# Attention's softmax sums: from a broadcast by matmul to a broadcast read back from DRAM

## The chip, the cores and the metric

The kernel runs on one core of a Trainium2 chip. A core has a matmul engine (TensorE, PE in the profile), three elementwise engines (VectorE is DVE, ScalarE is ACT, GpSimd is POOL) and a sync engine (SP) that here only issues DMA transfers. Each engine runs its own list of instructions in the order that was fixed when the program was built, and waits for the others through semaphores. The time is device microseconds (us) of one execution.

## The reference

Two layers over 1024 tokens of width 1024. Layer 0 mixes tokens with grouped-query attention (16 heads of 64, 4 key/value heads), layer 1 with a gated MLP over chunks; each is followed by a squared-ReLU MLP. The change lies in the end of the attention:

```python
s = jnp.einsum('bqkgd,bskd->bkgqs', q_blk, k).astype(jnp.float32) * scale
p = jax.nn.softmax(s, axis=-1).astype(v.dtype)
return jnp.einsum('bkgqs,bskd->bqkgd', p, v)
...
return o @ w_o
...
x = x + g1[:, None, :] * y
```

## The kernel before, in words

Activations are held transposed: width on the 128 partitions, in eight tiles `dt` (or `m`, `k`) of 128, and tokens along the free axis, in two halves `hf` of 512. Every large product is three matmuls: an operand is split into a high part (a cast to a shorter float, on ACT) and a low part (the rest, a subtraction on DVE or POOL), and high·high, high·low and low·high are added up in PSUM.

**Attention** runs as 64 units, one for each head and each 256 queries, in a software pipeline: at step `i` PE makes the scores of unit `i` (L948), transposes the exponentials of unit `i-1` (L965) and multiplies those of unit `i-1` and `i-2` with the values (L984). DVE takes the row maximum (L951) and the low parts (L974), ACT the exponentials (L957, which add up the row sums in `rowsum`) and the high parts (L968), POOL adds the two parts of a unit's output (L1001). These instructions are kept in program order by `pin`. The others, such as most of what is named below, are placed by the scheduler of the language, which moves an instruction among its neighbours as its readiness and the buffers allow. The exponentials are not divided by their sum at once. The unnormalized output of a head pair and half, `ot[(dt, hf)]` (128 x 512), is multiplied by the reciprocal sums later, in `wo_prep`. In between, at the `m` place of a unit, side work runs: the slabs (L184 to L200: weights loaded by SP, multiplied and summed on POOL) and `mod_ahead` (a weight column loaded on SP, L221, multiplied with the condition and summed on DVE one to two units later, L225).

**The reciprocal sums** in the kernel before: `wo_sums(hf)` takes the reciprocal of the 128 x 64 sums (L880), splits it in high and low (L882, L883), transposes it four times on PE into a 32 x 512 tile (L886), and ACT copies that out of PSUM (L888). `wo_prep(hf, dt)` then multiplies a 0/1 matrix `sel` with it on PE (L892), which puts each head's row on its 64 partitions in PSUM; DVE multiplies the attention output with that (L894), ACT takes the high part (L896) and POOL (first half) or DVE (second half) the low part (L897). `sel` is loaded (L869) and cast on ACT (L875) before. For the first half all this is spread over the units 53 to 62, one `dt` in each unit from 55 on; for the second half it stands between the output products.

**The output projection**, `wo_mm(m, halves, bank)`, has 24 matmuls for a half (L906 to L908), then DVE adds the gated result to `x` (L910), ACT squares it (L260) and DVE sums the squares (L264). Its weights come through `issue_w`: SP loads a tile of 128 x 1024 (L113), ACT casts the high part (L116), POOL subtracts for the low part (L117). `AHEAD = 1`, so `wo_mm(m)` issues the weights of `m + 1`: those that `wo_mm(3)` needs are asked for in `wo_mm(2)`. `WA = 6`: after the attention come `wo_mm(1)` to `wo_mm(5)` for the first half, `wo_mm(6)` and `(7)` for both, then `wo_mm(0)` to `(5)` for the second. `mods(n)` adds column loads with a multiplication on DVE (L145, L153) between them.

## Time and profile before

| | |
|---|---|
| time, median of 3 runs | 2628.07 us (2626.15 to 2628.24) |
| span of the profiled execution | 2625.8 us |
| PE busy | 2601.6 us, 99% of the span |
| DVE, ACT, POOL busy | 83%, 55%, 28% |
| granted TensorE clock, mean | 0.999 |
| units 53 to 63 and the end of attention | from about 470 to 555 us |
| output projection around the change | from about 548 to 582 us |

The profile is of one execution. Its span runs from the first to the last instruction; the median of the runs lies 2.3 us above it. Rows of the timeline begin with the start in us and the length in us, then engine, line, operation, output <- inputs, the number of instructions, and in brackets how long the engine had been idle before, and for what. Rows of the grouped views say busy us, mean ns of one, and idle time before.

### The profile page before, as it was taken

How to read it: one execution, taken by the hardware profiler on the slowest of the kernel's cores; microseconds unless marked ns; L12 is line 12 of the kernel's file. 1: busy time of each engine (PE TensorE's matmuls, PEld its weight loads, DVE VectorE, ACT ScalarE, POOL GpSimd, SP SyncE). 2: the span in 40 equal slices, each digit the busy share in tenths (PEclk: the TensorE clock that was granted, in tenths of full speed). 3: DMA queues.
4: the chain of work that ended last, by engine and by line, in shares of the span. 5: the costliest groups of instructions: out<-in, count | busy, mean ns of one | idle time of the engine just before them, and what ended most of it. 6: DMA issues, size and time to landing. Idle time of an engine off the chain costs nothing. (4 is left out here: it accounts for less than half of the span.)

```text
span 2625.8 us, 37307 instructions
## 1 busy us (share of the span) xinstructions
PE 2601.6 (99%) x12860; PEld 2172.2 (83%) x12860; DVE 2183.1 (83%) x3276; ACT 1451.1 (55%) x2612; POOL 723.2 (28%) x531
## 2 busy tenths in 40 slices
PE   9999999999999999999999999999999999999999
PEld 7789999888788888888888888888888788888887
DVE  7868999887989989877897687788979977789974
ACT  4569999854654455446543354445456645465442
POOL 0238776533000004430122054451520000005400
PEclk9999999999999999999999999999999999999999
DMA  8010222234486788545243355568641554487461
GB/s 306 27 33 9 74 88 75 97 112 145 168 288 245 270 310 306 192 133 172 82 136 121 120 174 175 178 204 305 237 141 50 177 179 156 153 310 268 149 211 58
DMA packets 208752, 435.39 MB, mean 166 GB/s; under 512 B 23025, under 2 KB 35441, under 8 KB 208562
## 3 DMA queue, kind: packets, MB, share of 16 engines
q1 hardware_dynamic: 181682, 395.24, 44.7%
q10 hardware_dynamic: 26880, 37.76, 4.0%
q8 instruction: 102, 1.67, 0.3%
q14 instruction: 88, 0.72, 0.1%
HBM read 310.23 MB, written 122.68 MB: 165 GB/s over the span
## 5 line engine op out<-in xcount | busy, mean ns | idle before, releaser
L1212 PE MATMUL out<-t,s 128*128 128x512 f32 x1232 | 479.9, 390 | 0.9 <-ACT t L328 0.8
L1213 PE MATMUL out<-t,s 128*128 128x512 f32 x1232 | 479.3, 389 | 0.7 <-DVE t L329 0.7
L1214 PE MATMUL out<-t,s 128*128 128x512 f32 x1232 | 478.9, 389 | 0.0
L469 PE MATMUL w<-t,s 128*128 128x512 f32 x1168 | 459.8, 395 | 0.9 <-ACT t L328 0.5
L470 PE MATMUL w<-t,s 128*128 128x512 f32 x1168 | 455.2, 390 | 1.8 <-DVE t L329 1.8
L471 PE MATMUL w<-t,s 128*128 128x512 f32 x1168 | 454.7, 389 | 0.0
L329 DVE TENSOR_TENSOR t<-t,t 128x512 fp32r<-128x512 f32 x408 | 324.7, 806 | 36.2 <-ACT t L328 29.0
L328 ACT CAST t<-t 128x512 fp32r<-128x512 f32 x408 | 245.3, 617 | 122.2 <-DMA t<-hf 71.7
L1213 PEld LDWEIGHTS out<-t,s 128*128 128x128 f32 x1232 | 231.2, 188 | 50.2 <-DVE t L329 1.8
L1212 PEld LDWEIGHTS out<-t,s 128*128 128x128 f32 x1232 | 231.2, 188 | 50.2 <-ACT t L328 1.7
L1214 PEld LDWEIGHTS out<-t,s 128*128 128x128 f32 x1232 | 231.2, 188 | 48.1
L454 ACT CAST s<-w 128x512 fp32r<-128x512 f32 x292 | 173.4, 616 | 161.4 <-PE w L471 104.3
L470 PEld LDWEIGHTS w<-t,s 128*128 128x128 f32 x1168 | 219.3, 188 | 49.7 <-DVE t L329 5.2
L469 PEld LDWEIGHTS w<-t,s 128*128 128x128 f32 x1168 | 219.3, 188 | 49.4 <-issue 2.9
L471 PEld LDWEIGHTS w<-t,s 128*128 128x128 f32 x1168 | 219.2, 188 | 45.6
L455 DVE TENSOR_TENSOR s<-w,s 128x512 fp32r<-128x512 f32 x292 | 221.8, 766 | 41.1 <-ACT s L454 40.6
L1194 ACT CAST s<-t 128x512 fp32r<-128x512 f32 x240 | 148.2, 620 | 187.0 <-PE out L1214 136.3
L1180 POOL TENSOR_TENSOR w<-w,t 128x512 f32<-128x512 f32 x20 | 34.2, 1721 | 767.7 <-DMA t<-hf 691.5
L1195 DVE TENSOR_TENSOR s<-t,s 128x512 fp32r<-128x512 f32 x240 | 195.1, 814 | 56.1 <-ACT s L1194 55.4
L951 DVE TENSOR_REDUCE mx<-s 128x1 f32<-128x1024 f32 x128 | 156.2, 1220 | 30.5 <-PE s L948 29.2
L974 DVE TENSOR_TENSOR t<-t,t 128x512 fp32r<-128x512 f32 x256 | 164.1, 681 | 17.1 <-ACT t L968 16.4
L984 PE MATMUL o<-t,t 128*128 128x256 f32 x1024 | 162.6, 291 | 0.0
(251 smaller groups left out, 5089.1 us busy)
## 6 DMA issues: line engine op xcount, KB each, us to landing
t<-hf SPq DMA_DIRECT2D x320, 256.0 KB, 4.0
hf<-c SPq DMA_DIRECT2D x156, 256.0 KB, 3.4
w<-in_wi_dram SPq DMA_DIRECT2D x64, 512.0 KB, 4.5
hf<-c ACTq DMA_DIRECT2D x96, 256.0 KB, 2.7
w<-in_ada_dram SPq DMA_DIRECT2D x36, 512.0 KB, 3.9
x<-in_ada_dram SPq DMA_DIRECT2D x64, 256.0 KB, 5.4
t<-in_wm_dram SPq DMA_DIRECT2D x64, 256.0 KB, 4.7
wf<-w SPq DMA_DIRECT2D x64, 256.0 KB, 3.0
```

Source lines behind the costliest of these rows:

```text
L328: S.copy(hi, src)
L329: (eng or V).tensor_tensor(lo, src, f32(hi), ALU.subtract)
L454: S.copy(hi, src)
L455: V.tensor_tensor(lo, src, f32(hi), ALU.subtract)
L469: T.matmul(ps, hi[:, a], th, start=kt == 0, stop=False)
L470: T.matmul(ps, hi[:, a], tl, start=False, stop=False)
L471: T.matmul(ps, lo[:, a], th, start=False, stop=kt == 3)
L974: pin(V.tensor_tensor(lo, pt, f32(hi), ALU.subtract))
L1195: V.tensor_tensor(lo, src, f32(hi), ALU.subtract)
L1212: T.matmul(ps, hi[:, a], th, start=begin and kt == 0, stop=False, **g)
L1213: T.matmul(ps, hi[:, a], tl, start=False, stop=False, **g)
L1214: T.matmul(ps, lo[:, a], th, start=False, stop=end and kt == 3, **g)
```

## The change

The broadcast by matmul goes. `wo_sums` keeps the reciprocal in one float32 piece, transposes it four times into a 16 x 512 tile, copies it on ACT and stores it from ACT's queue to a DRAM tile `rd`. A new function `wo_load(hf, dt)` issues two loads on SP's queue, each of which reads one row of `rd` for 64 partitions. `wo_prep` multiplies with that tile, which lies in SBUF and not in PSUM. `sel`, its load and its casts are gone. In the first half `wo_sums` moves from unit 54 to unit 49, the loads stand in units 51 to 58, and the products stay in units 55 to 62. In the second half the loads of a group of `dt` stand behind `wo_mm(m)`, and the products ahead of `wo_mm(m + 1)` and no longer of `wo_mm(m)`.

```diff
     def wo_sums(hf):
         ri = small.tile([P, 4, NH], F32, tag="ri", name=nm("ri"), bufs=1)
         V.reciprocal(ri, rowsum[:, 4 * hf : 4 * hf + 4])
-        rs = small.tile([P, 4, 2, NH], F32R, tag="rs", name=nm("rs"), bufs=1)
-        V.tensor_copy(rs[:, :, 0], ri)
-        V.tensor_tensor(rs[:, :, 1], ri, f32(rs[:, :, 0]), ALU.subtract)
-        pt = bank_x("rt", (32, 512), F32R)
+        pt = bank_x("rt", (NH, 512))
         for j in range(4):
-            T.transpose(pt[:, j * P : (j + 1) * P], rs[:, j].rearrange("p s h -> p (s h)"), identr)
-        rT[hf] = slot(F32R, (32, 512))
-        S.copy(rT[hf], f32(pt))
+            T.transpose(pt[:, j * P : (j + 1) * P], ri[:, j], ident)
+        rT = slot(F32, (NH, 512))
+        S.copy(rT, pt)
+        rd[hf] = dram.tile([NH, 512], F32, name=nm("rd"))
+        nc.scalar.dma_start(rd[hf], rT)
+
+    def wo_load(hf, dt):
+        rb_[(dt, hf)] = slot()
+        for i in range(2):
+            nc.sync.dma_start(rb_[(dt, hf)][64 * i : 64 * i + 64],
+                              rd[hf][2 * dt + i : 2 * dt + i + 1].broadcast_to([64, 512]))
 
     def wo_prep(hf, dt):
-        pb = bank_x("bc")
-        T.matmul(pb, sel[dt // 4][:, (dt % 4) * P : (dt % 4 + 1) * P], rT[hf], start=True, stop=True)
         o_ = ot.pop((dt, hf))
-        V.tensor_tensor(o_, o_, pb, ALU.mult)
+        V.tensor_tensor(o_, o_, rb_.pop((dt, hf)), ALU.mult)
...
                     if i in deferred:
                         deferred.pop(i)()
-                    elif i == WO_AT - 6:
-                        load_sel()
-                    elif WO_AT <= i < WO_AT + 10:
-                        if i == WO_AT:
-                            copy_sel()
-                        elif i == WO_AT + 1:
-                            wo_sums(0)
-                        else:
+                    elif i == WO_AT - 4:
+                        wo_sums(0)
+                    elif WO_AT - 2 <= i < WO_AT + 10:
+                        if i < WO_AT + 6:
+                            wo_load(0, i - WO_AT + 2)
+                        if i > WO_AT + 1:
                             wo_prep(0, i - WO_AT - 2)
...
     for m in range(1, WA):
         if m == 1:
             x[1] = [load_x(1, k) for k in range(KT)]
-        for dt in PREP[m - 1] if m < 4 else ():
+        for dt in PREP[m - 2] if 1 < m < 5 else ():
             wo_prep(1, dt)
         wo_mm(m, (0,), bank_y)
+        for dt in PREP[m - 1] if m < 4 else ():
+            wo_load(1, dt)
         mods(WOM[m])
```

Most line numbers move by it: L880 becomes L868, L886 L871, L888 L873, L894 to L897 become L885 to L888, L906 to L910 L897 to L901, L116 and L117 L117 and L118, L225 L226, L260 and L264 L261 and L265, L951 L942, L974 L965. New are the store L875 and the loads L880.

The scheduler places what is not pinned anew, so two places that the diff doesn't name change their order.

The first is DVE's list in attention, in unit 47. In the kernel before, this stands there at a row maximum of that unit (`mx_5500`), with the multiplication of the column that `mod_ahead` loads into `w_5581` two units behind it:

```order
L974 TENSOR_TENSOR t_5476<-t_5467,t_5472 128x512
L951 TENSOR_REDUCE mx_5500<-s_5495 128x1
L974 TENSOR_TENSOR t_5521<-t_5507,t_5512 128x512
L951 TENSOR_REDUCE mx_5537<-s_5532 128x1
L974 TENSOR_TENSOR t_5539<-t_5523,t_5528 128x512
L974 TENSOR_TENSOR t_5548<-t_5541,t_5546 128x512
```

```order
L974 TENSOR_TENSOR t_5702<-t_5686,t_5691 128x512
L974 TENSOR_TENSOR t_5711<-t_5704,t_5709 128x512
L974 TENSOR_TENSOR t_5726<-t_5717,t_5722 128x512
L225 SCALAR_TENSOR_TENSOR w_5581,mod<-w_5581,s_110 128x1024
L226 TENSOR_TENSOR mod<-mod,cols 128x1
L166 SCALAR_TENSOR_TENSOR amod<-mod,cols 128x1
```

Now the same place reads so (the column is named `w_5579` here):

```order
L965 TENSOR_TENSOR t_5478<-t_5469,t_5474 128x512
L942 TENSOR_REDUCE mx_5502<-s_5497 128x1
L226 SCALAR_TENSOR_TENSOR w_5579,mod<-w_5579,s_112 128x1024
L965 TENSOR_TENSOR t_5523<-t_5509,t_5514 128x512
L942 TENSOR_REDUCE mx_5539<-s_5534 128x1
L965 TENSOR_TENSOR t_5541<-t_5525,t_5530 128x512
```

The column's multiplication (L225, now L226) has moved up, from behind the three low parts of a later unit to right behind the row maximum `mx_5502`, ahead of a low part that attention waits for.

The second place is the output projection, on ACT. `wo_mm(2)` adds to `x_6947` (now `x_6948`), and `wo_mm(3)` uses the weights `s_7226` (now `s_7206`), `wo_mm(4)` `s_7280` (now `s_7270`), `wo_mm(5)` `s_7320` (now `s_7326`). Before:

```order
L896 CAST t_7140<-t_4466 128x512
L896 CAST t_7147<-t_4634 128x512
L896 CAST t_7154<-t_4804 128x512
L116 CAST s_7226<-w_7224 128x1024
L260 ACTIVATE t_7190<-x_6945 128x512
L896 CAST t_7206<-t_4968 128x512
L896 CAST t_7213<-t_5148 128x512
L116 CAST s_7280<-w_7278 128x1024
L896 CAST t_7220<-t_5316 128x512
L260 ACTIVATE t_7256<-x_6947 128x512
L896 CAST t_7267<-t_5486 128x512
L116 CAST s_7320<-w_7318 128x1024
```

Now:

```order
L261 ACTIVATE t_7167<-x_6946 128x512
L887 CAST t_7190<-t_4468 128x512
L887 CAST t_7195<-t_4636 128x512
L887 CAST t_7200<-t_4806 128x512
L261 ACTIVATE t_7236<-x_6948 128x512
L117 CAST s_7206<-w_7204 128x1024
L887 CAST t_7254<-t_4970 128x512
L887 CAST t_7259<-t_5150 128x512
L887 CAST t_7264<-t_5318 128x512
L117 CAST s_7270<-w_7268 128x1024
L261 ACTIVATE t_7300<-x_6950 128x512
L887 CAST t_7315<-t_5488 128x512
```

The cast of the weights for `wo_mm(3)` stood ahead of the square of `x_6945`, the result of `wo_mm(1)`. Now it stands behind the square of `x_6948`, the result of `wo_mm(2)`. In the rows behind these the cast for `wo_mm(5)` likewise stands behind the square of `wo_mm(4)`'s result.

The third is DVE's list at the same place. Before:

```order
L894 TENSOR_TENSOR t_4466<-t_4466,bc_7137 128x512
L894 TENSOR_TENSOR t_4634<-t_4634,bc_7144 128x512
L894 TENSOR_TENSOR t_4804<-t_4804,bc_7151 128x512
L897 TENSOR_TENSOR t_7141<-t_4466,t_7140 128x512
L897 TENSOR_TENSOR t_7148<-t_4634,t_7147 128x512
L897 TENSOR_TENSOR t_7155<-t_4804,t_7154 128x512
L910 SCALAR_TENSOR_TENSOR x_6945<-wo_7164,mod,x_6945 128x512
```

Now:

```order
L901 SCALAR_TENSOR_TENSOR x_6946<-wo_7141,mod,x_6946 128x512
L265 TENSOR_TENSOR t_7060<-t_7060,t_7167 128x512
L885 TENSOR_TENSOR t_4468<-t_4468,t_7170 128x512
L901 SCALAR_TENSOR_TENSOR x_6948<-wo_7210,mod,x_6948 128x512
L888 TENSOR_TENSOR t_7191<-t_4468,t_7190 128x512
L885 TENSOR_TENSOR t_4636<-t_4636,t_7173 128x512
L885 TENSOR_TENSOR t_4806<-t_4806,t_7176 128x512
L888 TENSOR_TENSOR t_7196<-t_4636,t_7195 128x512
L888 TENSOR_TENSOR t_7201<-t_4806,t_7200 128x512
```

The products of the first three tiles stood ahead of the addition of `wo_mm(1)`'s result (L910, `x_6945`); now two of the three stand behind that of `wo_mm(2)` (L901, `x_6948`).

## The prediction

> **What bounds the kernel now.** I read the page first, then the waits of PE over the whole span, then the timeline around the change.

> ```profile
> span 2625.8 us, 37307 instructions
> PE 2601.6 (99%) x12860; PEld 2172.2 (83%) x12860; DVE 2183.1 (83%) x3276; ACT 1451.1 (55%) x2612; POOL 723.2 (28%) x531
> ```

> PE is busy 99% of the span. What leaves PE's list is a gain where PE has enough to eat, and whatever makes PE wait is a loss in full, since nothing behind it has slack. The waits of PE (us in total, times, longest) are small:

> ```profile
> PE t L965 <- ACT c L957: 2.4, 3, 1.9
> PE qkv L575 <- DVE t L635: 2.1, 1, 2.1
> PE wo L908 <- POOL s L117: 0.2, 1, 0.2
> ```

> In the output projection PE waited 0.2 us for weights once. So the question is what PE loses in matmuls, and what it gains in waits.

> **What the change removes.** The first term is the eight broadcasts of the first half. PE's timeline has a unit without one (from 470.09 to 475.60) and a unit with one (from 513.15 to 519.58), which also has a transpose of queries:

> ```profile
> 470.09 1.09 PE L948 MATMUL s<-x,t 128*128 128x512 f32 x4
> 475.60 1.09 PE L948 MATMUL s<-x,t 128*128 128x512 f32 x4
> ...
> 513.15 1.20 PE L948 MATMUL s<-x,t 128*128 128x512 f32 x4
> 515.00 0.53 PE L934 MATMUL qt<-identr,t 128*128 128x128 f32 x4
> 515.38 0.62 PE L965 MATMUL t<-ident,c 128*128 128x128 f32 x4
> 519.15 0.49 PE L892 MATMUL bc<-t,t 32*128 32x512 f32 x1
> 519.58 1.20 PE L948 MATMUL s<-x,t 128*128 128x512 f32 x4
> ```

> 6.43 - 5.51 - 0.38 for the query transposes is 0.54 us a broadcast, 4.3 us for eight. But ACT is nearly full in these units. The stretch 508 to 527 (the columns are stretch, length, and busy us of PE, weight loads, DVE, ACT and POOL, then granted clock and DMA) holds 2.95 such units:

> ```profile
> 508.00:527.00 19.00, 19.00 (x134) 16.68 (x133) 16.62 (x22) 17.90 (x36) 6.01 (x6) 1.00 0.26 84
> ```

> ACT idles 1.10 us there, 0.37 a unit; when PE gives back more, ACT sets the pace. So 8 x 0.37 = 3.0 us, with 2.4 (0.3 a unit, not all idle time being usable) and 4.3 as bounds. **-3.0.**

> The two casts of `sel` go from ACT. They stood ahead of a copy of the query transposes for which PE idled 0.33 us: **-0.3.**

> ```profile
> 477.33 1.14 ACT L875 CAST t<-t 32x512 fp32r<-32x512 f32 x2
> ```

> ```profile
> 479.62 0.66 PE L965 MATMUL t<-ident,c 128*128 128x128 f32 x4 [0.33 <-ACT t L937]
> ```

> Unit 57 has the longest wait of attention: ACT stood 2.27 us before the first weight cast, whose load had not landed, and PE ran out of exponentials. Behind it the clock was halved.

> ```profile
> 497.85 1.05 ACT L116 CAST s<-w 128x1024 fp32r<-128x1024 f32 x1 [2.27 <-DMA w<-in_wo_dram]
> ```

> ```profile
> 500.55 1.59 PE L965 MATMUL t<-ident,c 128*128 128x128 f32 x7 [1.89 <-ACT c L957]
> ```

> ```profile
> 115.06:118.47 3.41, 3.41 (x10) 2.64 (x9) 3.41 (x5) 0.08 (x1) 3.25 (x4) 0.50 0.00 0
> 500.77:504.18 3.41, 3.41 (x14) 2.92 (x13) 1.40 (x3) 3.40 (x7) 3.41 (x7) 0.50 0.46 119
> ```

> The two longest waits of PE, 2.1 and 1.89 us, were both followed by 3.41 us at half clock, worth up to 1.7 us each. In the new order both casts stand a few instructions later, so part of this goes: all of it is 1.89 + 1.7 = 3.6, nothing is the other bound. I take **-1.5**.

> In the second half the matmuls stand in three groups (3, 3 and 2) between the output products, with nothing to hide behind. The middle one:

> ```profile
> 562.11 0.39 PE L908 MATMUL wo<-t,s 128*128 128x512 f32 x1
> 562.43 0.96 PE L892 MATMUL bc<-t,t 32*128 32x512 f32 x3
> 563.32 0.51 PE L906 MATMUL wo<-t,s 128*128 128x512 f32 x1
> 563.67 0.40 PE L907 MATMUL wo<-t,s 128*128 128x512 f32 x1
> 563.90 0.40 PE L908 MATMUL wo<-t,s 128*128 128x512 f32 x1
> ```

> From 562.11 to 563.67 two steps took 1.56 us instead of 2 x 0.23: 1.10 us. Three groups: **-3.3**. The transposes of the sums are four before and after. Removed in all: 8.1 us, between 6.0 and 11.5.

> **What it moves.** Two new orders cost PE time. The first is the column's multiplication in attention, which now follows the row maximum directly.

> ```profile
> 438.06 0.35 SPq L221 DMA_DIRECT2D w<-in_ada_dram  x1
> ```

> ```profile
> w<-in_ada_dram SPq DMA_DIRECT2D x1, 512.0 KB, 4.2
> ```

> ```profile
> 438.50 0.69 DVE L974 TENSOR_TENSOR t<-t,t 128x512 fp32r<-128x512 f32 x1
> 453.51 1.22 DVE L225 SCALAR_TENSOR_TENSOR w<-w,s 128x1024 f32<-128x1024 f32 x1
> ```

> ```profile
> 440.28 0.60 PE L965 MATMUL t<-ident,c 128*128 128x128 f32 x4
> ```

> Its column is issued at 438.06 and lands 4.2 us later, at 442.3; before, it was used at 453.5. DVE would stand until then, multiply until 443.5, and finish the low part of 438.50 at 444.2 and not 439.2. PE's transposes at 440.28 to 440.6 need the PSUM bank which that low part reads, so PE waits 3.5 us or so: between 2.7, with a landing 0.8 us sooner, and 5.5, if a POOL addition holds DVE off as below. After a wait of this length the clock fell both times: 1.5 more. **+5.0**, from 2.7 to 7.2.

> The second, and the largest term, is the weights of the output projection. What the parts take there, from the groups by line between 543 and 600 us:

> ```profile
> L117 POOL TENSOR_TENSOR s<-w,s 128x1024 fp32r<-128x1024 f32 x6 | 16.1, 2676 | 30.4 <-ACT s L116 25.5 <-PE bc L892 4.8
> L116 ACT CAST s<-w 128x1024 fp32r<-128x1024 f32 x6 | 6.3, 1051 | 14.8 <-DMA w<-in_wo_dram 8.5 <-PE wo L907 6.3
> L910 DVE SCALAR_TENSOR_TENSOR x<-wo,mod,x 128x512 f32<-128x512 f32 x8 | 6.0, 744 | 3.9 <-PE wo L908 3.9
> L897 DVE TENSOR_TENSOR t<-t,t 128x512 fp32r<-128x512 f32 x8 | 5.3, 683 | 0.0
> L896 ACT CAST t<-t 128x512 fp32r<-128x512 f32 x8 | 4.9, 621 | 6.4 <-DVE t L894 6.4
> L260 ACT ACTIVATE t<-x 128x512 f32<-128x512 f32 x7 | 4.4, 634 | 9.4 <-DVE x L910 9.2
> ```

> Count from the end of `wo_mm(2)`. DVE adds its result (0.74), takes a low part and multiplies two tiles (three at about 0.63 when they follow each other); ACT casts the last tile (0.62), squares (0.63), and only then casts the weights of `wo_mm(3)` (1.05): 4.9 us, in which PE has nothing, because `wo_mm(3)` is next in its list. Then POOL makes the low part (2.4 in the row at 563.49 below) while PE has two matmuls of 0.23: 1.95 more. 6.9 us. For `wo_mm(4)` the cast stands behind three more casts of products that DVE reaches late; by the same rows its high part comes as `wo_mm(3)` ends, and the low part 1.95 later: 2.0. For `wo_mm(5)` it stands behind the square of `wo_mm(4)`: 0.74 + 0.63 + 1.05 = 2.4, and 1.95: 4.4. **+13.3.** The lower bound is 11: neighbours overlap by 0.1 each, and the wait of `wo_mm(4)` halves. The upper is 16: POOL takes the mean of 2.68 each time, and the high part for `wo_mm(4)` comes 2 us late.

> These waits are as long as those after which the clock fell. A half-clock stretch is partly spent in the next wait, so I count 2.0 for three of them, from 0 to 5. **+2.0.** [...]

> The product now reads two SBUF tiles. DVE instructions of that kind stretch where POOL subtracts:

> ```profile
> 564.40 2.05 DVE L264 TENSOR_TENSOR t<-t,t 128x512 f32<-128x512 f32 x1
> ```

> ```profile
> 563.49 2.42 POOL L117 TENSOR_TENSOR s<-w,s 128x1024 fp32r<-128x1024 f32 x1 [4.83 <-PE bc L892]
> ```

> An instruction of this size takes 0.68 otherwise (L897 above); this one lasted until POOL's ended, to within 0.6 us. The products stand in just that chain. [...] One such meeting on the chain costs up to 1.4, and not every one lies on it: **+0.8**, from 0 to 2.7.

> The store and the 32 new loads cost nothing by themselves. In the first half they are issued two units and more ahead of their product. In the second the reciprocals leave ACT where L888 stood; with 2.7 us for a store from ACT's queue and under 4 for a load of SP's, all three tiles land before `wo_mm(2)` ends. What that cover is worth is a rival below.

> ```profile
> hf<-c ACTq DMA_DIRECT2D x96, 256.0 KB, 2.7
> t<-hf SPq DMA_DIRECT2D x320, 256.0 KB, 4.0
> ```

> **The sum.** -8.1 + 5.0 + 13.3 + 2.0 + 0.8 = +13.0 us. On the span of 2625.8 that is 2638.8; the median of the runs lies 2.3 above the span, so 2641.

> **The rivals.** First, the waits are shorter and the clock stays: -8.1 + 2.7 + 12 = +6.6, 2635. For it speaks that a half-clock stretch has been seen only twice; against it, that both times the wait was shorter than these.

> Second, the broadcasts through DRAM come late. A product whose tile has not landed holds DVE, behind it the low parts, and then PE. SP issues in order, and in the second half its loads of broadcasts and of weights stand in one queue; a landing 2 us later in each of the three groups gives +6 more, 2647. Against it: the margin of about 3 us in the second half and of two units in the first.

> Third, the other side: the work taken from PE decides. If the weights' casts were still ready when `wo_mm(3)` to `(5)` begin, only -8.1 would be left, 2620, or 2625 with the wait in attention. The point from which it decides is 8.1 us: the new waits together must stay under that. For it speaks that PE is the bound; against it, that the cast waits in ACT's list for a result which PE itself gives just ahead of needing it. No timing can hide that.

> **Chances.** Forecast 0.62, first rival 0.16, second 0.12, third 0.10. A change within 0.2% (5.3 us) is about what a measurement here can't tell from none: the third rival falls on both sides of it, and the low end of the first reaches into it. Faster 0.07, same 0.09, slower 0.84. The terms' bounds, not all at one end at once, give 2633 to 2650; taking in part of the rivals, the range is 2629 to 2651.

> **What would show it.** In the changed profile: PE waiting on the cast of the weights (L117) some 5 us once and 2 to 3 us once, and on POOL's low part (L118) about 2 us three times; PE waiting near 440 us for a low part (L965), with DVE idle before L226 for its DMA; half clock behind these; units 55 to 62 shorter by 0.3 to 0.4 us with ACT full. It is wrong if PE's waits in the projection add up to less than 8 us, or if DVE waits for the broadcast loads.

## The result, and the profile after

| | before | changed |
|---|---|---|
| median | 2627.11 us (2623.98 to 2628.24, 4 runs) | 2650.55 us (2647.84 to 2652.16, 4 runs) |
| ratio to before, 95% interval | | 1.0089 (1.0078 to 1.0101) |
| span of the profiled execution | 2625.8 us | 2646.1 us |

The change makes the kernel 0.9% slower, 23.4 us by the medians. The forecast was 2641 us. The profiled execution of the changed kernel is its shortest (2647.84 us), 20.3 us of span above that of before; the accounts below are made between these two. One execution of e4 below took 3232.91 us at a mean granted clock of 0.752, and its median leaves it out.

The page's first part and the waits of PE over the span, of the changed kernel:

```profile
span 2646.1 us, 37342 instructions
PE 2601.1 (98%) x12844; PEld 2173.4 (82%) x12844; DVE 2193.1 (83%) x3272; ACT 1449.3 (55%) x2610; POOL 724.7 (27%) x531
```

```profile
PE t L956 <- DVE t L965: 13.1, 8, 5.2
PE wo L897 <- ACT s L117: 9.4, 2, 7.0
PE wo L899 <- POOL s L118: 3.3, 3, 1.7
```

PE has 16 matmuls fewer and is busy as long as before, since its busy time is also longer where the clock is halved (a matmul of the output projection shows 0.63 us there and 0.39 otherwise). The wait for the weights' casts is new. That for POOL's low parts was 0.2 us before, and that for low parts in attention, now 13.1, was this:

```profile
PE t L965 <- DVE t L974: 2.9, 4, 1.1
```

Between 430 and 610 us there was none of it before; 10.2 of the 13.1 lie there now, in four waits. The columns of the next rows are stretch, length, busy us of PE, weight loads, DVE, ACT and POOL, then granted clock and DMA:

```profile
441.40:448.20 6.80, 3.54 (x15) 3.35 (x16) 5.72 (x7) 2.36 (x5) 1.50 (x1) 0.50 0.21 77
564.95:577.52 12.57, 5.60 (x25) 4.32 (x24) 8.78 (x15) 4.05 (x6) 0.00 (x0) 0.88 0.90 271
577.52:587.32 9.80, 8.53 (x25) 6.36 (x25) 8.87 (x13) 2.78 (x4) 4.59 (x2) 0.63 0.70 227
587.32:595.98 8.66, 5.92 (x26) 4.25 (x24) 6.69 (x11) 3.44 (x5) 0.86 (x1) 1.00 0.32 114
595.98:605.10 9.12, 7.42 (x25) 5.70 (x25) 7.66 (x10) 1.04 (x1) 4.84 (x2) 0.81 0.61 184
```

The last four are `wo_mm(2)` to `wo_mm(5)`, from first matmul to first matmul of the next. They take 40.15 us; before, with the broadcasts between them, these four took 22.77. The clock was halved for 6.8 us near 441, for 10.2 from 574.5 and for 3.4 from 598.4.

The early wait, first DVE and then PE:

```profile
441.80 2.18 DVE L226 SCALAR_TENSOR_TENSOR w<-w,s 128x1024 f32<-128x1024 f32 x1 [4.45 <-DMA w<-in_ada_dram]
```

```profile
444.65 1.11 PE L956 MATMUL t<-ident,c 128*128 128x128 f32 x4 [5.25 <-DVE t L965]
```

DVE stood 4.45 us before the column's multiplication because the column had not landed, and the multiplication took 2.18 us instead of 1.22. PE waited 5.25 us for the low part behind it.

The weights of `wo_mm(3)`, on ACT:

```profile
573.70 0.62 ACT L261 ACTIVATE t<-x 128x512 f32<-128x512 f32 x1
576.42 1.04 ACT L117 CAST s<-w 128x1024 fp32r<-128x1024 f32 x1 [2.10 <-DMA w<-in_wo_dram]
```

The cast stands behind the square, as the order said. But behind the square ACT waited 2.10 us more, for the load. That load was issued late. SP's list had stood 16.2 us at the first broadcast load, which waits for the store of the sums; then came that group's six loads, two columns, and only then the weights:

```profile
SPq L880 <- DMA rd<-t: 16.2, 1, 16.2
```

```profile
562.55 3.65 SPq L880 DMA_DIRECT2D t<-rd  x6
566.30 1.00 SPq L146 DMA_DIRECT2D w<-in_ada_dram  x2
567.41 0.38 SPq L114 DMA_DIRECT2D w<-in_wo_dram  x1
```

This is 2.46 us behind the start of `wo_mm(2)`. Before, the same tile was asked for 5.45 us ahead of that start:

```profile
557.87 0.33 SPq L113 DMA_DIRECT2D w<-in_wo_dram  x1
```

The load was also slow to land. The transfers from 562 to 580 us show it, and the same view before, from 560 to 582, stands below it (packets' share of the 16 DMA engines 77% now; the rows give count, size and median us from issue to landing):

```profile
t<-rd SPq DMA_DIRECT2D x16, 128.0 KB, 5.8
w<-in_ada_dram SPq DMA_DIRECT2D x4, 512.0 KB, 5.8
w<-in_wo_dram SPq DMA_DIRECT2D x2, 512.0 KB, 7.5
```

```profile
w<-in_wo_dram SPq DMA_DIRECT2D x3, 512.0 KB, 3.3
w<-in_ada_dram SPq DMA_DIRECT2D x3, 512.0 KB, 3.4
```

The 7.5 us are the middle of two: the tile for `wo_mm(3)` took 8.9 us to land and the next 6.1; before, these loads took 3.2 to 3.7. An estimate from these numbers: landing in 3.3 us the tile would have been there at 570.7, and issued 2.1 us sooner it would have been there at the square's end, 574.3. So it took the late issue and the slow landing together. And in unit 53, DVE and POOL:

```profile
477.42 2.73 DVE L885 TENSOR_TENSOR t<-t,t 128x512 f32<-128x512 f32 x1
```

```profile
477.21 2.38 POOL L201 TENSOR_TENSOR s<-s,w 128x1024 f32<-128x1024 f32 x1
```

The first product, no longer tied to a matmul, had floated two units ahead, stood in front of a row maximum, and met an addition on POOL: 2.73 us for an instruction of 0.68.

### The profile page after: what moved, and what is told of

It is laid out like the page before. It is cut to its first block, busy times and chain, and to the rows that moved or that the text cites. A ratio compares the mean times of both kernels' runs of the same rounds, so it can differ in the third digit from the quotient of the medians.

```text
span 2646.1 us, 37342 instructions
## 1 busy us (share of the span) xinstructions
PE 2601.1 (98%) x12844; PEld 2173.4 (82%) x12844; DVE 2193.1 (83%) x3272; ACT 1449.3 (55%) x2610; POOL 724.7 (27%) x531
## 5 line engine op out<-in xcount | busy, mean ns | idle before, releaser
L942 DVE TENSOR_REDUCE mx<-s 128x1 f32<-128x1024 f32 x128 | 155.9, 1218 | 28.4 <-PE s L939 27.3
L965 DVE TENSOR_TENSOR t<-t,t 128x512 fp32r<-128x512 f32 x256 | 164.1, 680 | 18.5 <-ACT t L959 17.9
L956 PE MATMUL t<-ident,c 128*128 128x128 f32 x1024 | 150.5, 275 | 13.9 <-DVE t L965 13.1
## 6 DMA issues: line engine op xcount, KB each, us to landing
t<-hf SPq DMA_DIRECT2D x320, 256.0 KB, 3.9
hf<-c SPq DMA_DIRECT2D x156, 256.0 KB, 3.5
w<-in_wi_dram SPq DMA_DIRECT2D x64, 512.0 KB, 4.4
hf<-c ACTq DMA_DIRECT2D x96, 256.0 KB, 2.2
w<-in_ada_dram SPq DMA_DIRECT2D x36, 512.0 KB, 4.5
x<-in_ada_dram SPq DMA_DIRECT2D x64, 256.0 KB, 5.8
t<-in_wm_dram SPq DMA_DIRECT2D x64, 256.0 KB, 4.8
wf<-w SPq DMA_DIRECT2D x64, 256.0 KB, 3.0
```

The lines of the kernel that those rows point to most:

```text
L965: pin(V.tensor_tensor(lo, pt, f32(hi), ALU.subtract))
```

## The experiments

All ratios are to the kernel before on the same chip, with 95% intervals.

| run | what | median us | ratio |
|---|---|---|---|
| e1 | change, reciprocal pinned | 2646.42 | 1.0068 (1.0051 to 1.0085) |
| e2 | change, waits filled with matmuls | 2651.44 | 1.0090 (1.0075 to 1.0105) |
| e3 | before, casts in the changed order | 2640.01 | 1.0051 (1.0034 to 1.0068) |
| e4 | change, orders put right | 2632.28 | 1.0020 (1.0010 to 1.0029) |
| e5 | DRAM in the first half alone | 2624.13 | 0.9990 (0.9981 to 0.9999) |
| e6 | e4, sums in unit 48, weights further ahead | 2625.41 | 0.9999 (0.9990 to 1.0008) |
| e7 | e6, four column loads later | 2630.29 | 1.0014 (1.0006 to 1.0023) |
| e8 | before, 16 added loads | 2636.68 | 1.0041 (1.0027 to 1.0055) |
| e9 | e5, first weight casts in units 59, 60 | 2622.20 | 0.9982 (0.9973 to 0.9991) |
| e10 | all of it, columns spread | 2627.56 | 1.0000 (0.9991 to 1.0009) |
| e11 | before, first weight casts in units 59, 60 | 2625.15 | 0.9991 (0.9982 to 0.9999) |
| e12 | e10, columns spread otherwise | 2624.06 | 0.9991 (0.9982 to 1.0000) |

### e1: the lost pin

`pin` ties an instruction to the one that was written ahead of it on its engine. The column's multiplication is written in unit 49, and the change puts the unpinned reciprocal, whose inputs are ready since unit 32, right ahead of it.

```diff
-        V.reciprocal(ri, rowsum[:, 4 * hf : 4 * hf + 4])
+        r_ = V.reciprocal(ri, rowsum[:, 4 * hf : 4 * hf + 4])
+        if hf == 0:
+            pin(r_)
```

> The changed kernel with one edit: the reciprocal of the first half's sums is pinned behind the VectorE instruction written before it. The column's multiplication of unit 47's load is pinned to whatever VectorE instruction is written ahead of it; in the changed kernel that is this unpinned reciprocal, which floats forward and lets it go. Theory (the lost pin): the multiplication stands in unit 49 again, PE's wait of 5.2 us near 440 us and the half clock behind it go, and the time is 6 to 8 us below the changed kernel's, about 2643. Rival (the column's load lands late because of other transfers in the change): PE still waits 3 us or more near there, and the time moves by less than 2 us.

The wait of 5.25 us is gone from unit 47, and the half clock with it; units 47 and 48 take 5.85 and 5.51 us, and took 12.46 and 6.19. So the lost pin is the cause. The median fell by 4.1 us only (2650.55 to 2646.42), less than forecast, and the intervals of the two ratios overlap; between the two profiles the span fell by 8.8. One cost of the pin is seen, a wait of its own, since the transposes now stand in the same unit as the reciprocal:

```profile
PE rt L873 <- DVE ri L868: 1.4, 1, 1.4
```

### e2: the waits filled

`fill(n)` issues `n` matmuls of a constant with a tile of 128 x 512 into a PSUM bank that nobody reads.

```diff
+    FM = (3,)
...
+            if halves == (0,) and m in FM and m != 4:
+                fill(28 if m == 3 else 10)
             for k in range(KT):
                 hi, lo = on[(k, hf)]
                 T.matmul(ps[hf], wh[:, k], hi, start=k == 0, stop=False)
                 T.matmul(ps[hf], wh[:, k], lo, start=False, stop=False)
+                if halves == (0,) and m in FM and k == 0:
+                    fill(8)
```

> The changed kernel with 36 extra matmuls of the same size whose result nobody reads, in the places where PE waits for the weights of wo_mm(3): 28 ahead of it (6.4 us), 8 between its second and third matmul (1.8 us). They add work and take none away. Theory (the clock): PE keeps busy through the wait, the clock stays at 1.00 in wo_mm(3) where the changed kernel had a mean of 0.63, and the time falls by 2 to 4 us although PE does 8 us more. Rival (the clock's fall costs nothing, since the next weights are late anyway): the same time or up to 1 us longer.

The clock did what was expected, the time did not. `wo_mm(3)` with its eight fillers ran at full clock:

```profile
580.84:589.33 8.49, 7.41 (x33) 5.82 (x32) 7.55 (x14) 2.79 (x4) 1.25 (x1) 1.00 0.85 259
```

But `wo_mm(2)` to `(5)` took 41.7 us instead of 40.15. A wait of 1.08 and one of 2.38 us came into `wo_mm(4)`, which had 0.30 in the changed kernel: its weights are late by their own chain, and the slow `wo_mm(3)` had only hidden that. The wait in unit 57, which the edit doesn't touch, was 4.0 us in this execution and 2.7 in the changed kernel's. That the halved clock cost time in `wo_mm(3)` is not shown; the rival holds there.

### e3: the order alone

```diff
-        S.copy(hi, raw)
-        G.tensor_tensor(lo, raw, f32(hi), ALU.subtract)
+        def cast():
+            c_ = S.copy(hi, raw)
+            if held[0] is not None:
+                pin(c_)
+            G.tensor_tensor(lo, raw, f32(hi), ALU.subtract)
+        if held[0] is None:
+            cast()
+        else:
+            held[0].append(cast)
...
+        held[0] = [] if halves == (0,) and m in (2, 4) else None
         wh, wl = load_w("wo", m)
...
             (sqA, sqB)[hf].add(x[hf][m])
+        for c_ in held[0] or ():
+            c_()
+        held[0] = None
```

> The kernel before, broadcast by matmul and all, with one edit: ScalarE's casts of the weights of wo_mm(3) and wo_mm(5) stand behind the squares of wo_mm(2)'s and wo_mm(4)'s results, as they do in the changed kernel. No transfer is added. Theory (the order alone makes the waits): 0.74 + 0.63 + 1.05 us until the high part and 1.95 more until the low part, 4.4 us each, two of them, and 1 to 3 us of half clock: 9 to 12 us above the kernel before, 2636 to 2639. Rival (the transfers through DRAM make the waits, and the order would be harmless without them): less than 2 us above.

It lost 12.7 us (2640.01 against 2627.28), a little more than forecast. The waits, two for the high and two for the low part:

```profile
PE wo L915 <- ACT s L118: 4.4, 2, 2.4
PE wo L917 <- POOL s L121: 3.7, 2, 1.9
```

They are 8.2 us, 8.8 were forecast, and `wo_mm(3)` and `(5)` ran at mean clocks of 0.67 and 0.66. No transfer had been added. So the order is enough to make such waits.

### e4: the orders put right

```diff
         wo_mm(m, (0,), bank_y)
+        if m < 5:
+            pinned[0] = True
+            issue_w()
+            pinned[0] = False
         for dt in PREP[m - 1] if m < 4 else ():
             wo_load(1, dt)
...
-        for dt in PREP[m - 2] if 1 < m < 5 else ():
+        for dt in PREP[m - 3] if 2 < m < 6 else ():
             wo_prep(1, dt)
```

What `issue_w()` asks for there are the weights of `wo_mm(m + 2)`. The casts of these and of the second half's products are pinned, the first half has e1's pin, and its products are pinned too.

> The change with its order put right: the reciprocal and the first half's products pinned in their units; in the second half the weights of wo_mm(m + 2) asked for right behind wo_mm(m) and ahead of the broadcast loads, their casts pinned behind the square of wo_mm(m), and the products another step later, their casts pinned behind those of the weights. Theory (only the orders cost, and the matmuls taken away are worth what was forecast): no wait over 1 us between 430 and 600 us but that of unit 57, and 5 to 9 us below the kernel before, 2618 to 2622. Rival (the 32 loads and their queue cost by themselves): waits for weights or broadcasts stay, and the time is not below the kernel before.

18 us of the 23 are back, but the time is not below the kernel before: the rival holds for the second half. The wait ahead of `wo_mm(3)` is gone; its weights were now loaded back in attention. Behind the squares of the next steps ACT still stood, now for the loads alone:

```profile
569.84 1.05 ACT L117 CAST s<-w 128x1024 fp32r<-128x1024 f32 x1 [3.53 <-DMA w<-in_wo_dram]
576.53 1.06 ACT L117 CAST s<-w 128x1024 fp32r<-128x1024 f32 x1 [3.54 <-DMA w<-in_wo_dram]
```

These two loads took 8.0 and 6.6 us to land. They were issued at 561.71 and 569.81 and the squares ended at 566.3 and 573.0, so with the 3.3 us of before (an estimate) ACT would have stood for 0.1 us at most: here it is the landing that costs. In the first half the pin on the products worked: unit 53 takes 5.51 us and unit 54 8.23, and with e1's pin alone they took 6.61 and 9.35. In this execution 1.56 us of that went again in unit 55, which ran partly at half clock (7.47 us and not 5.91); e5, with the same pin, has 5.91 there.

### e8: the loads alone

```diff
+            pinned[0] = halves == (0,) and m > 0
             (sqA, sqB)[hf].add(x[hf][m])
+            pinned[0] = False
...
         wo_mm(m, (0,), bank_y)
+        for dt in PREP[m - 1] if m < 4 else ():
+            spare = slot()
+            for i in range(2):
+                nc.sync.dma_start(spare[64 * i : 64 * i + 64],
+                                  t["rope"][0, 2 * dt + i : 2 * dt + i + 1].broadcast_to([64, 512]))
         mods(WOM[m])
```

> The kernel before, broadcast by matmul and all, with 16 added loads of 128 KB in the second half where the changed kernel has its own, each reading one row of another input for 64 partitions; nobody reads what they bring. ScalarE's squares there are pinned behind the weights' casts, so that the order of the changed kernel does not come about. Theory (the transfers alone hold up the weights): the weights land 6 to 8 us after their issue and not 3.3, PE waits 1 to 3 us for them two or three times, 4 to 9 us above the kernel before. Rival (the added loads are free, only the order costs): within 2 us of it.

In the kernel before, broadcast by matmul, 16 loads that nobody reads and the pins cost 10.2 us (2636.68 against 2626.46), a little more than forecast. PE waited 1.73 and 2.13 us in `wo_mm(4)` and 1.22 and 1.70 in the step behind `wo_mm(5)`. Between 560 and 585 us:

```profile
w<-in_wo_dram SPq DMA_DIRECT2D x2, 512.0 KB, 5.4
```

But the theory's reason, a slow landing, is not what made these waits. The 5.4 us are the middle of 3.7, for the weights of `wo_mm(4)`, and 7.1, for those of `wo_mm(5)`, for which PE did not wait; those of the step behind it took 3.5. What was late for `wo_mm(4)` is the issue: the load stood 9.4 us in SP's list for a column's multiplication on DVE (columns and weights share four buffers), until 572.82, where before it was issued at 565.93, ahead of `wo_mm(3)`:

```profile
SPq L113 <- DVE mod L158: 9.4, 1, 9.4
```

```profile
572.82 0.33 SPq L113 DMA_DIRECT2D w<-in_wo_dram  x1
```

```profile
565.93 0.33 SPq L113 DMA_DIRECT2D w<-in_wo_dram  x1
```

So loads that are added to SP's list, with the pins, are enough to make such waits, by the order in which things are issued. That their transfers do it is not shown here, and no run has the pins alone.

### e6 and e7: what the transfers compete with

e6 is e4 with the sums moved from unit 49 to unit 48, where no pinned multiplication follows, in place of the pin, and weights asked for ahead up to `wo_mm(7)`.

> As the fourth run, with the sums of the first half taken in unit 48 and not pinned in unit 49, and the weights of all of wo_mm(3) to (7) asked for ahead. The columns' multiplications between the output products are where they were. Theory (the transfers are too many for the stretch): the weights of wo_mm(4) and (5) still land 7 us or more after their issue, PE waits 1 to 2 us for each of them, and the time is 2 to 5 us below the fourth run, about 2629. Rival (the waits of the fourth run came of its order alone): no wait over 0.5 us, 2620.

No wait in unit 49 was left, the weights landed in 6.0 us, and PE waited 1.84, 1.07 and 1.46 us for low parts: 2625.41, no difference from before that can be measured. That is between the theory's 2629 and the rival's 2620.

```diff
-WOM = (0, 2, 1, 1, 2, 3, 4, 1)
+WOM = (0, 0, 0, 0, 2, 4, 6, 2)
```

> As the run with the sums in unit 48 beside this one, with one edit: of the 14 column loads of 512 KB between the output products, the four that stood behind wo_mm(1) to (3) stand behind wo_mm(5) to (7) instead, so 2 MB less is moved while the broadcasts and the weights are. Theory (the transfers are too many for the stretch): the weights land in 4 to 5 us, the waits of wo_mm(3) to (5) go, 3 to 6 us below that run and 4 to 8 us below the kernel before, 2619 to 2623. Rival (the order of ScalarE's list makes the waits): the same time as that run, within 1 us.

The weights landed as fast as in the kernel before (the rows are of 550 to 575 us):

```profile
t<-rd SPq DMA_DIRECT2D x16, 128.0 KB, 4.1
w<-in_wo_dram SPq DMA_DIRECT2D x3, 512.0 KB, 3.2
```

But they did not land beside all the broadcasts. With no column in front of them, the weights of `wo_mm(4)` to `(6)` were all issued ahead of the first broadcast load, the last two just before it, where in e6 those of `wo_mm(4)` stood behind six of these loads. Those of `wo_mm(7)` were issued at 573.80, behind the last:

```profile
552.25 0.80 SPq L114 DMA_DIRECT2D w<-in_wo_dram  x2
553.16 3.64 SPq L882 DMA_DIRECT2D t<-rd  x6
```

`wo_mm(2)` to `(4)` took 5.44 us each without a wait; in `wo_mm(5)` one of 1.42 was left. So the waits go when the columns are moved, as the theory said, but e7 does not tell fewer transfers from an earlier place in SP's list. The time it forecast did not come: the run is slower than e6. The columns that now stand behind `wo_mm(4)` to `(6)` are ahead of the next step's weights in SP's list, and PE waited for these:

```profile
PE wo L903 <- ACT s L117: 3.9, 1, 3.9
```

### e5, e9 and e11: the first half alone

In e5 the second half is that of the kernel before: `wo_sums1` and `wo_prep1` are its functions.

```diff
-                    elif i == WO_AT - 4:
+                    elif i == WO_AT - 5:
                         wo_sums(0)
...
-        V.tensor_tensor(o_, o_, rb_.pop((dt, hf)), ALU.mult)
+        p_ = V.tensor_tensor(o_, o_, rb_.pop((dt, hf)), ALU.mult)
+        if hf == 0:
+            pin(p_)
...
-    wo_sums(1)
+    copy_sel()
+    wo_sums1(1)
```

> The DRAM route in the first half alone, with the sums taken in unit 48 (no pin is lost there) and the first half's products pinned in their units; the second half has the broadcast by matmul again, its 0/1 matrix loaded in unit 59 and cast at the end of attention. Theory (in the first half the route is worth what the matmuls cost, in the second it is not, since its loads hold up the weights): no wait for weights over 0.5 us in wo_mm(1) to (5), units 55 to 62 some 0.5 us shorter each, 4 to 6 us below the kernel before, 2621 to 2623. Rival (the loads cost attention as much as the matmuls did): within 2 us of the kernel before.

There was no wait of note in the output projection, and units 59 to 62 take 5.83, 5.51, 5.51 and 5.51 us (6.43, 6.11, 6.13 and 6.10 before). But the time is only 2.3 us below, 0.1%. Unit 57 took 11.51 us: ACT reaches the first weight cast sooner than its load lands.

```profile
500.32 1.04 ACT L117 CAST s<-w 128x1024 fp32r<-128x1024 f32 x1 [3.00 <-DMA w<-in_wo_dram]
```

```profile
504.30 1.12 PE L993 MATMUL t<-ident,c 128*128 128x128 f32 x4 [4.61 <-DVE t L1002]
```

e9 moves these two casts:

```diff
+                    if i in (59, 60):
+                        pinned[0] = True
+                        issue_w()
+                        pinned[0] = False
                     if late_mods and i % 4 == 1:
```

> The DRAM route in the first half alone, as in the fifth run, and the casts of the first two tiles of output weights asked for and pinned in units 59 and 60, where their loads have long landed, and no longer in unit 57. Theory (what is left of that run's cost is the wait of 4.6 us in unit 57 and the half clock behind it): no wait over 1 us between 430 and 600 us, 6 to 9 us below the kernel before, 2617 to 2620. Rival (ScalarE is so full in these units that a cast costs its full time in any of them): 2 to 4 us below the kernel before, as the fifth run.

5.0 us below the kernel before (2622.20 against 2627.23), the fastest of all; less than forecast, more than the rival. PE's longest wait between 430 and 600 us is 0.7. ACT is now busy 44.54 of 45 us there, and PE 43.30:

```profile
495.00:540.00 45.00, 43.30 (x312) 38.77 (x311) 40.65 (x56) 44.54 (x89) 19.91 (x18) 1.00 0.33 98
```

e11 has the same edit on the kernel before.

> The kernel before with one edit: the casts of the first two tiles of output weights asked for and pinned in units 59 and 60. It tells how much of the ninth run's gain is the route through DRAM. Theory: the wait of 1.9 us in unit 57 and its half clock go, but ScalarE gets a microsecond of cast in each of two units that have 0.4 us free: 1 to 3 us below the kernel before. Rival (all of the ninth run's gain is in the place of the casts): 6 us or more below.

2.1 us below, as forecast. So of e9's 5.0 us some 3 are the DRAM route: 2622.20 against 2625.15, beside the same runs of before, though the intervals of the two ratios overlap. The profiles agree: units 47 to 62 take 95.7 us in e9, 99.0 in e11 and 102.1 before.

### e10 and e12: both halves

e10 is e6 with e9's casts, the weights behind `wo_mm(6)` asked for ahead of its columns, and `WOM = (0, 0, 0, 0, 3, 3, 4, 4)`; e12 has `(0, 0, 0, 1, 3, 3, 5, 2)`.

> The DRAM route in both halves with all that the runs so far asked for: sums in unit 48, products pinned, weights ahead of the broadcast loads, weight casts in units 59 and 60, no column load behind wo_mm(1) to (4), and the weights of wo_mm(0)'s second half asked for ahead of wo_mm(6)'s columns. Theory (orders and transfers were all that stood against the change): no wait over 1.5 us between 430 and 620 us, 8 to 12 us below the kernel before, 2614 to 2618, and below the first half alone by the 3 us of the second half's matmuls. Rival (the column loads only move the jam on): a new wait of 2 us or more for weights behind wo_mm(5), and not below the first half alone.

> As the tenth run, with the 14 column loads spread otherwise: none behind wo_mm(0) to (2), one behind wo_mm(3), then 3, 3, 5 and 2. In the tenth run the wait had moved to about 617 us, where ScalarE's forms of the norm stood behind two casts of late weights. Theory (a spread exists in which weights, broadcasts and columns all arrive): no wait over 1.5 us between 430 and 640 us, 8 to 11 us below the kernel before, 2616 to 2619. Rival (the stretch holds more transfers than it has time for, wherever they stand): a wait of 2 us or more for weights or for the norm, and not below the first half alone, about 2622.

The rival holds in e10, though the wait is not for weights itself: it had moved to the norm's broadcast near 617 us, 4.1 us. ACT stood there for a result of POOL, which had a subtraction of late weights ahead of it in its list:

```profile
616.32 1.28 ACT L287 ACTIVATE t<-ident,r 128x128 f32<-128x128 f32 x4 [2.50 <-POOL r L245]
```

In e12 one wait of 3.2 us was left, in `wo_mm(5)` and of another kind, so its rival's sign came too. DVE ran eight instructions on two SBUF tiles back to back (0.68 us each, from 567.42 to 572.31), and POOL's subtraction for these weights, begun at 569.18, took 5.34 us instead of 2.4:

```profile
569.18 5.34 POOL L120 TENSOR_TENSOR s<-w,s 128x1024 fp32r<-128x1024 f32 x1 [4.10 <-ACT s L117]
```

Neither beats the first half alone. That no spread of the columns does is not shown; two were tried.

## Why the prediction was right, and where it was not

The sign held, and so did the main mechanism, two new orders that make PE wait. The size was 13.0 us where 23.4 came (20.3 between the profiles), and the median lies only half a microsecond inside the range, which ended at 2651.

| term | forecast | between the profiles |
|---|---|---|
| eight broadcasts and unit 57 (units 55 to 62) | -3.0 - 1.5 | -4.9 |
| units 49 to 54: casts of `sel`, products meeting POOL | -0.3 + 0.8 | +2.1 |
| wait for the column, with its half clock (units 47, 48) | +5.0 | +7.3 |
| second half's broadcasts (`wo_mm(1)` to `(3)`) | -3.3 | -3.1 |
| waits for weights, `wo_mm(3)` to `(5)` | +13.3 | +12.7 |
| half clock in these, and what is left | +2.0 | +5.7 |

(The row of the weights' waits adds up 6.97 + 1.27 + 0.30 + 2.44 + 1.70. The last row is what is left of the 40.15 us when 4 x 5.44 of matmuls and the waits are taken off. PE worked 9.3 us in the two half-clock stretches there, of which half, 4.6, is the clock's part. The sum is 19.8; half a microsecond lies elsewhere.)

**What held.** Six of the seven units other than 57 are 0.5 to 0.6 us shorter (unit 58 by 0.08), a little more than ACT's idle time let one expect. Over units 59 to 62 that idle time fell from 0.42 to 0.07 us a unit, 0.35 of the 0.57 gained; where the rest comes from is not shown. One of these units, from scores to scores:

```profile
524.83 1.09 PE L939 MATMUL s<-x,t 128*128 128x512 f32 x4
530.34 1.09 PE L939 MATMUL s<-x,t 128*128 128x512 f32 x4
```

5.51 us, and 6.11 before. The order of the casts makes the waits (e3), and the moved multiplication the one in attention (e1). DVE's multiplication (2.18 us, 1.22 before) met POOL's addition there, which the upper bound of that term had allowed for: 5.25 us.

```profile
440.57 2.34 POOL L201 TENSOR_TENSOR s<-s,w 128x1024 f32<-128x1024 f32 x1
```

Neither of the two signs against it came: PE's waits in the projection add up to 12.7 us, and DVE waited for no broadcast load.

**What was right by luck.** The waits for weights come out right as a sum (13.3 and 12.7), not in their parts: 6.9, 2.0 and 4.4 were forecast for `wo_mm(3)` to `(5)`, and 8.2, 0.3 and 4.1 came. Unit 57 became 1.4 us shorter, its broadcast included, but not by a shorter wait, for which 1.5 was counted: PE's wait there grew from 1.89 to 2.72 us. What went is the half clock behind it, and that was chance; the last section shows why. In e1 and e2 the same unit has waits of 2.10 and 4.03, the latter with half clock.

**What was mis-sized.** The half clock was taken as 2.0 with 5 as its bound and is 5.7 by the account, 4.6 of it seen in the trace; e2 shows that one part of it, in `wo_mm(3)`, is no cost of its own, but the lateness of the next weights under another name. The meeting of products with POOL was taken as 0.8 and cost about 2 (e4, with the products pinned, is 1.10 and 1.12 us shorter than e1 in units 53 and 54): the step that failed is the one that looked for it only in the output projection, while the first product met POOL in attention, in front of a row maximum.

**What failed.** "The store and the 32 new loads cost nothing by themselves." The chain for `wo_mm(3)` was counted as 4.9 + 1.95; it was 7.0 + 1.3, since the weights' load ended 2.1 us after the square. The step counted when the broadcasts land, and neither that SP's list stands until the store has landed (16.2 us), with the weights behind, nor what 2 MB of broadcasts do to the landing of weights beside them. e4 shows the slow landing apart from the order on ACT, e8 the late issue. How much of the 2.1 us each makes is not shown by a run. The second rival had the loads late for their products; what was late was the weights.

The third rival, that the removed matmuls decide, is true of the first half once its orders are right (e9), and there it is worth some 3 us.

## What to carry to other kernels

Work on the bound engine was replaced by transfers: that paid some 3 us where the DMA engines were a third busy (0.33 in e9's stretch), and did not where they were busy for 0.6 to 0.9 of `wo_mm(2)`, `(3)` and `(5)`. Count such transfers against every other load of the stretch, by the time of landing and by the place in the issuing engine's list: a load that waits for a store keeps all that stands behind it from being issued, here for 16.2 us. Where a scheduler places what is not pinned, an added instruction can free a pinned one: read the order of each engine for what has moved, not only for what was added. An in-order queue makes a late operand everyone's wait (in e5 ACT stood 3.00 us for a load, and PE 4.61 us behind it), so casts of operands for the next step stand best where their loads have long landed.

## What the runs showed of the hardware

These are readings of the profiles of this case's runs.

DVE and POOL each took longer beside the other: DVE's product took 2.73 us instead of 0.68 in the changed kernel, beside a POOL addition of 2.38 us; POOL's subtraction took 5.34 instead of 2.4 in e12, beside DVE's row of products and low parts.
